# Where layer 0's later modulation vectors are made: five chunks on TensorE with summed tiles between them, three chunks at the feed-forward's entry

## The chip, the cores and the metric

The kernel runs on one core of a Trainium2 chip. The metric is the time of one execution in microseconds on the device. The engines that matter here are TensorE (PE in the profile, with PEld for its weight loads), VectorE (DVE), ScalarE (ACT), GpSimd (POOL) and SyncE (SP), whose queue issues most of the transfers. Each engine carries out its own list of instructions strictly in that list's order and waits at semaphores for the others.

## The reference, cut to what matters

Two transformer layers over 512 latent tokens and 256 context tokens, with a model width of 1024. Layer 0 has latent attention and neighbourhood attention side by side, layer 1 has sliding-window attention, and each is followed by a SwiGLU feed-forward. Every layer needs six modulation vectors of 1024 numbers for the latent stream (from `c`) and, in layer 0, as many again for the context stream (from `c_ctx`):

```python
for l in range(DEPTH):
    sh_a, sc_a, g_a, sh_f, sc_f, g_f = jnp.split(silu_c @ mod_w[l] + mod_b[l], 6, axis=-1)
    csh_a, csc_a, cg_a, csh_f, csc_f, cg_f = jnp.split(silu_cc @ mod_w[l] + mod_b[l], 6, axis=-1)
    a_lat = modulate(h_lat, sh_a, sc_a)            # rms_norm(h) * (1 + scale) + shift
    ...                                            # o_lat, o_ctx: the layer's attention and its output projection
    h_lat = h_lat + g_a * o_lat
    h_lat = h_lat + g_f * swiglu(modulate(h_lat, sh_f, sc_f), ffn_w_gate_up[l], ffn_w_down[l])
    ...                                            # the same for h_ctx while there is a layer after this one
return rms_norm(h_lat, final_norm)
```

In the order of that split the components are numbered 0 (attention shift), 1 (attention scale), 2 (attention gate), 3 (feed-forward shift), 4 (feed-forward scale) and 5 (feed-forward gate). Component (0, 3) is thus needed when the feed-forward of layer 0 modulates its input, and (0, 5) only when that feed-forward adds its output to the residual, far later.

## The kernel before, in words

All weights come in float32. A product with a weight tile is made of three matmuls on float32r parts: high weight by high data, high by low, low by high. ACT casts the high part of a weight tile (L332, in the feed-forward L1594), DVE subtracts it for the low part (L333, in the feed-forward L1595), and three PE lines of a helper (L345 to L347, L800 to L802, L1607 to L1609) make the products into PSUM tiles named `pss`, `psd`, `pst` and `pso`. A scheduler that simulates a timeline sets each engine's order from the program text; stretches of PE inside `in_order(...)` keep the order of the text.

The stages, with the time in the profiled execution at which each begins: the first modulation vectors and the entry norm; layer 0's input projections (60 us); the neighbourhood and the latent attention (184 us); the output projection and the norm that follows it; the feed-forward of layer 0, whose entry begins with the first gate-and-up products at 440 us and whose first down product is at 517.87 us; the rest of that feed-forward; layer 1; the last norm.

**The making of the modulation.** `all_mods` is a generator that makes one small piece at each step. `bg(n)` takes n steps of it; other work calls it at places that the text lists. `mod(...)` returns a finished vector and takes steps until it is there. There are three kinds of step:

- A PE chunk (`mods_pe`) makes 256 numbers of a component for both streams: four transfers of 256 KB from `mod_wp` on SP's queue into two `ph` and two `pl` tiles, matmuls with the conditioning (L202), an ACT copy (L204), matmuls that pick the two streams (L209), and two small DVE operations that add the bias (L216). Components (0, 4) and (0, 5) are made thus, in four chunks each.
- A summed tile makes 128 numbers in two steps. The first loads 256 KB into a `ph` and a `pl` tile and lets DVE multiply and sum them for the latent stream (L258). The second does that for the context stream by POOL (L275) and ACT (L276). Components (0, 2) and (0, 3) have 16 such tiles, 32 steps.
- A late tile is a single step, used from the end of the attention on: POOL's queue loads 512 KB (L229), in turn into one `rope` tile or into two `nb` tiles, and DVE sums (L236) and adds the bias (L241). Layer 1's components are made thus.

In the projections `bg` takes 37 steps in all (0.43 for each yield of the projections' loop, from the ninth on). Then it takes none until the output projection is done. In the feed-forward of layer 0, `bg(2)` is called at the second and third pair of gate-and-up blocks (j = 1 and 2), and `bg(more(j))` after that.

Before, the generator takes one PE chunk and then four summed steps, eight times over. The 37 steps of the projections thus hold all eight chunks and 29 of the 32 summed steps. Of the last three, one stands at the beginning of the attention; the last tile of (0, 3), number 7, is a late tile for both streams. Its two `nb` transfers are issued on POOL's queue at 256.56 us, and DVE works on it at the entry of the feed-forward. The four steps of j = 1 and 2 are then four late tiles of layer 1's component 1.

**The entry of the feed-forward.** `modulated_to` makes the input: DVE multiplies by the scale (L1533), ACT adds the shift (L1534), ACT and DVE split the result (L1594, L1595). The columns named "far" are begun before the norm's sum of squares is whole: `begun` starts products with `order[:4]` and `order[4:]` of the eight row blocks, the first with unnormalised data. The sum goes through `inverse`, a reciprocal (L1710) and `spread_to` (PE L474); then `norm.use` modulates the near columns, and the products of `near` run on PE in a written order. Pairs 1 to 3 follow. Weights of a pair are two `wr` tiles of 512 KB (one for gate, one for up) loaded by SP; a pair's sums and differences for a seven-product scheme (L1628, L1629, L1632, L1636 on DVE) go into `ph` and `pl` tiles, the same four-deep pools that the chunks and the summed tiles use. After the third pair `down0` begins with the first L345.

Of the kernel before, what the change touches and what calls it, by code (L numbers as in the profile page):

```python
# [102 lines left out]
def hybrid_kernel(ctx: ExitStack, tc, I, out):  # L103
# [189 lines left out]
    def component(l, comp):  # L293
        if (l, comp) in PE_MODS:
            yield from mods_pe(l, comp, PG if dense[0] else PQ)
            return
        for m in range(KT):
            yield from mod_tile(l, comp, m, (0, 1))

    def all_mods():  # L300
        by_pe, summed = (chain(component(0, a), component(0, b)) for a, b in ((4, 5), (2, 3)))
        for _ in by_pe:
            yield
            for _ in islice(summed, 4):
                yield
        yield from summed
        for comp in (1, 0):
            yield from component(1, comp)
        for comp in (2, 4, 3, 5):
            for m in range(KT):  # L310
                yield from mod_tile(1, comp, m, (0,))

    mods = all_mods()

    def bg(n=1):
# [1677 lines left out]
    norm, ops, sums, _ = combined(H, 1, 3, *HALVES)  # L1993
# [176 lines left out]
```

## Time and profile before

| | |
|---|---|
| median of 3 runs | 1563.93 us (1563.3 to 1567.26) |
| profiled execution | 1566.7 us, its span 1564.9 us |
| granted clock, mean | 0.992 |
| busy: PE, DVE, ACT, POOL | 97%, 75%, 52%, 18% of the span |
| projections, 60 to 184 us: PE busy | 123.22 of 124 us |
| entry of the feed-forward, 452 to 518 us: PE busy | 56.28 of 66 us |
| the longest wait of PE there | 5.74 us, ended at 457.75 us |

A row of the timeline reads: start in us, duration in us, engine, line, operation, output tile <- input tiles, shape; in square brackets the idle time of the engine ahead of it and what ended that. Neighbouring matmuls overlap in their ends, so the time that a matmul takes on PE is read from the distance of two starts. A row of the windows gives, for one stretch, its length, the busy time of PE, PEld, DVE, ACT and POOL with the number of instructions in brackets, the granted clock of PE as a share of full speed, the share of the transfer engines, and GB/s.

### The profile page before, as it was taken

To read this page: it belongs to the slowest core of one execution; us is meant where nothing else is said; L and a number is where in the kernel's file an instruction comes from. 1 tells how busy PE (TensorE), PEld (TensorE's weight loads), DVE (VectorE), ACT (ScalarE), POOL (GpSimd) and SP (SyncE) were. 2 spreads that over 40 slices of the span, in tenths; PEclk is the share of its full clock that TensorE was granted. 3 is DMA by queue.
4 is the path that set the end of the run, shared out by engine and by line. 5 is a ranking of instruction groups with operands and counts; after the bars stand their busy time and mean duration, and the time that the engine had idled before them with its cause. 6 is when DMAs were issued, how large, how long until landed. Compare 5 with 4: busy or idle time off the path is not lost.

```text
span 1564.9 us, 26627 instructions
## 1 busy us (share of the span) xinstructions
PE 1525.5 (97%) x9968; PEld 1358.2 (87%) x9968; DVE 1175.1 (75%) x2362; ACT 809.1 (52%) x1630; POOL 280.8 (18%) x317
## 2 busy tenths in 40 slices
PE   9999999999989999999999999999999999999998
PEld 6687767887988999898999999877789999898997
DVE  5896586666699497876877777888877679678686
ACT  5564587676564243242433345557757445354453
POOL 0264434332000010111111110381011000000000
PEclk9999999999999999999999999999999999999999
DMA  9585362004442554746666655140015223324222
GB/s 336 197 239 186 93 166 80 11 6 176 151 159 76 193 183 149 247 161 211 202 217 226 219 180 197 42 145 4 2 56 161 71 82 125 115 75 135 87 90 88
DMA packets 80849, 216.63 MB, mean 138 GB/s; under 512 B 10704, under 2 KB 17744, under 8 KB 80720
## 3 DMA queue, kind: packets, MB, share of 16 engines
q1 hardware_dynamic: 65200, 162.49, 32.2%
q0 software_dynamic: 13216, 49.29, 9.2%
q10 hardware_dynamic: 2304, 3.15, 0.5%
q8 instruction: 78, 1.28, 0.3%
q14 instruction: 51, 0.42, 0.1%
HBM read 187.10 MB, written 23.07 MB: 134 GB/s over the span
## 4 chain that ended last, share of the span: by engine, by line
PE 81%; DVE 8%; DMA 5%; issue 4%; ACT 2%; POOL 0%; SPq 0%; DVEq 0%; POOLq 0%; ACTq 0%
PE pso L557 5%; PE pss L345 4%; PE pss L346 4%; PE pss L347 4%; PE pss L1609 4%; PE psd L345 4%; PE pss L1607 4%; PE pss L1608 4%; PE psd L346 4%; PE psd L347 4%; PE psd L1609 3%; PE psd L1607 3%; PE psd L1608 3%; PE pss L789 3%; PE pst L504 3%
## 5 line engine op out<-in xcount | busy, mean ns | idle before, releaser
L332 ACT CAST wh<-wr 128x512 fp32r<-128x512 f32 (+2 forms) x139 | 105.9, 776 | 202.8 <-PE pss L346 64.5
L333 DVE TENSOR_TENSOR wl<-wr,wh 128x512 fp32r<-128x512 f32 (+2 forms) x136 | 126.3, 936 | 64.8 <-ACT wh L332 64.2
L563 ACT ACTIVATE p<-p,sm 128x512 f32<-128x512 f32 (+3 forms) x144 | 105.0, 730 | 27.7 <-DVE sm L567 26.7
L1607 PE MATMUL pss<-b,wh 128*128 128x384 f32 (+1 forms) x300 | 93.3, 311 | 0.0
L1608 PE MATMUL pss<-b,wh 128*128 128x384 f32 (+1 forms) x300 | 93.2, 311 | 0.0
L1609 PE MATMUL pss<-b,wl 128*128 128x384 f32 (+1 forms) x300 | 92.7, 312 | 0.0
L346 PE MATMUL psd<-b,wh 128*128 128x512 f32 (+3 forms) x249 | 84.3, 339 | 0.0
L1609 PE MATMUL psd<-b,wl 128*128 128x384 f32 (+1 forms) x248 | 78.9, 318 | 4.4 <-DVE wl L1595 4.4
L1608 PE MATMUL psd<-b,wh 128*128 128x384 f32 (+1 forms) x248 | 78.4, 316 | 0.0
L1607 PE MATMUL psd<-b,wh 128*128 128x384 f32 (+1 forms) x248 | 78.3, 316 | 0.0
L557 PE MATMUL pso<-ph,b 128*64 128x256 f32 (+1 forms) x400 | 76.9, 351 | 0.6 <-DVE ph L495 0.5
L557 PE MATMUL pso<-pl,b 128*64 128x256 f32 (+1 forms) x400 | 77.0, 351 | 0.1
L345 PE MATMUL psd<-b,wh 128*128 128x512 f32 (+3 forms) x209 | 73.6, 353 | 0.5 <-DVE b L495 0.5
L345 PE MATMUL pss<-st,wh 128*128 128x512 f32 (+2 forms) x212 | 72.6, 342 | 0.0
L347 PE MATMUL psd<-b,wl 128*128 128x512 f32 (+3 forms) x209 | 72.5, 348 | 0.0
L789 PE MATMUL pss<-st,st 128*128 128x512 f32 (+2 forms) x264 | 68.2, 372 | 4.3 <-DVE sm L567 4.1
L347 PE MATMUL pss<-st,wl 128*128 128x512 f32 (+2 forms) x212 | 72.2, 341 | 0.0
L346 PE MATMUL pss<-b,wh 128*128 128x256 f32 (+3 forms) x215 | 70.6, 329 | 0.0
L1594 ACT CAST wh<-ph 128x512 fp32r<-128x512 f32 x80 | 46.3, 619 | 44.8 <-DVE ph L1629 16.3
L1594 ACT CAST wh<-wr 128x1024 fp32r<-128x1024 f32 x40 | 42.0, 1050 | 42.0 <-PE pss L346 10.4
L1594 ACT CAST wh<-pl 128x512 fp32r<-128x512 f32 x80 | 46.0, 619 | 30.5 <-PE pst L1608 10.6
L504 PE MATMUL pst<-ident_r,p 128*128 128x128 f32 x346 | 57.8, 276 | 2.3 <-ACT p L563 1.2
(676 smaller groups left out, 5334.6 us busy)
## 6 DMA issues: line engine op xcount, KB each, us to landing
wr<-in_w_gu_dram SPq DMA_DIRECT2D x88, 512.0 KB, 4.1
wr<-in_w_out_dram SPq DMA_DIRECT2D x32, 512.0 KB, 3.7
wr<-in_w_dn_dram SPq DMA_DIRECT2D x64, 256.0 KB, 2.8
p<-home SPq DMA_DIRECT2D x40, 384.0 KB, 4.6
home<-p POOLq DMA_DIRECT2D x40, 384.0 KB, 4.6
nb<-in_mod_w_dram POOLq DMA_DIRECT2D x50, 256.0 KB, 3.6
rope<-in_mod_w_dram POOLq DMA_DIRECT2D x24, 512.0 KB, 3.9
wr<-in_w_in_dram SPq DMA_DIRECT2D x21, 512.0 KB, 4.3
```

Source lines behind the costliest of these rows:

```text
L332: S.copy(h, r)
L333: (G if eng else V).tensor_tensor(lo, r, f(h), op=ALU.subtract)
L345: PE.matmul(o, wh[:, k], mh[:, c], start=first and k == 0, stop=False)
L346: PE.matmul(o, wh[:, k], ml[:, c], start=False, stop=False)
L347: PE.matmul(o, wl[:, k], mh[:, c], start=False, stop=last and k == n - 1)
L557: ins = PE.matmul(o[64 * i : 64 * i + 64, c], v(kt), t, start=n == 0, stop=n == len(moving[i]) - 1)
L563: S.activation(p[:, c], p[:, c], AF.Exp, bias=nm, scale=-1.0, accum_out=dn)
L789: PE.matmul(o, x, k, start=i == 0, stop=i == 1)
L1594: S.copy(h, t)
L1607: PE.matmul(o, wh, xh, start=first and k == 0, stop=False, skip_group_check=not first)
L1608: PE.matmul(o, wh, xl, start=False, stop=False, skip_group_check=not first)
L1609: PE.matmul(o, wl, xh, start=False, stop=k == 3, skip_group_check=not first)
```

## The change

The turn in `all_mods` becomes one chunk and seven summed steps, for five chunks; the rest of the summed steps follow, and then the three chunks that are left.

```diff
         by_pe, summed = (chain(component(0, a), component(0, b)) for a, b in ((4, 5), (2, 3)))
-        for _ in by_pe:
+        for _ in islice(by_pe, 5):
             yield
-            for _ in islice(summed, 4):
+            for _ in islice(summed, 7):
                 yield
         yield from summed
+        yield from by_pe
         for comp in (1, 0):
             yield from component(1, comp)
```

Nothing else of the text is changed; from there on the lines of the file carry a number that is higher by one (L1595 before is L1596 now). The 37 steps of the projections now hold five chunks and all 32 summed steps, so component (0, 3) is whole when the attention begins. The steps of j = 1 and 2 at the feed-forward are now the last three chunks of (0, 5) and one late tile of layer 1, and each later late tile comes three steps later.

On DVE, at the entry of the feed-forward, ahead of the first products of the norm: `nb`, `cond` and `mod` in the rows of L236 are the late tile of (0, 3). Before:

```order
L1595 TENSOR_TENSOR pl_5303<-wr_5275,ph_5302 128x512
L236 ISA p_5013,mod_315_1519<-nb_5009,cond_67 128x512
L236 ISA mod_315_1519 128x1
L1710 RECIPROCAL sm_5060<-sm_5060 128x3
L236 ISA p_5015,mod_315_1519<-nb_5010,cond_67,mod_315_1519 128x512
L236 ISA mod_315_1519 128x1
L236 ISA p_5018,mod_316_1520<-nb_5009,cond_67 128x512
L236 ISA mod_316_1520 128x1
L241 SCALAR_TENSOR_TENSOR mod_315_1519<-mod_315_1519,modb_76 128x1
L1628 TENSOR_TENSOR pl_5411<-wr_5400 128x512
L236 ISA p_5020,mod_316_1520<-nb_5010,cond_67,mod_316_1520 128x512
L236 ISA mod_316_1520 128x1
```

Now, on DVE at the same place:

```order
L1596 TENSOR_TENSOR pl_5234<-wr_5206,ph_5233 128x512
L1589 TENSOR_TENSOR p_4994<-b_4685 128x384
L1589 TENSOR_TENSOR p_4999<-b_4772 128x384
L1589 TENSOR_TENSOR p_5004<-b_4859 128x384
L1589 TENSOR_TENSOR p_5009<-b_4945 128x384
L1711 RECIPROCAL sm_4991<-sm_4991 128x3
L1596 TENSOR_TENSOR st_4996<-p_4994,st_4996 128x384
L1596 TENSOR_TENSOR st_5001<-p_4999,st_5001 128x384
L1596 TENSOR_TENSOR b_5006<-p_5004,b_5006 128x384
L1596 TENSOR_TENSOR b_5011<-p_5009,b_5011 128x384
L1534 SCALAR_TENSOR_TENSOR p_5062<-b_4264,mod_183_848,pso_5026 128x384
```

The sums of the late tile and its two bias additions are gone from here, the split of pair 2 (L1628) stands later, and the norm's multiplications follow the reciprocal at once.

On SP's queue, the transfers of the weights at the same entry; `in_w_gu` is gate and up, `in_w_dn` is down, `in_mod_wp` is a chunk's weights. Before:

```order
L136 DMA wr_5399<-in_w_gu_dram 128x1024
L136 DMA wr_5400<-in_w_gu_dram 128x1024
L136 DMA wr_5554<-in_w_gu_dram 128x1024
L136 DMA wr_5555<-in_w_gu_dram 128x1024
L136 DMA wr_5689<-in_w_dn_dram 128x512
```

Now:

```order
L136 DMA ph_5268<-in_mod_wp_dram 128x512
L136 DMA pl_5270<-in_mod_wp_dram 128x512
L136 DMA wr_5359<-in_w_gu_dram 128x1024
L136 DMA wr_5527<-in_w_gu_dram 128x1024
L136 DMA ph_5272<-in_mod_wp_dram 128x512
L136 DMA pl_5274<-in_mod_wp_dram 128x512
L136 DMA ph_5292<-in_mod_wp_dram 128x512
L136 DMA pl_5294<-in_mod_wp_dram 128x512
L136 DMA ph_5296<-in_mod_wp_dram 128x512
L136 DMA pl_5298<-in_mod_wp_dram 128x512
L136 DMA wr_5528<-in_w_gu_dram 128x1024
L136 DMA wr_5662<-in_w_dn_dram 128x512
```

Twelve chunk transfers have come in (the last four stand behind these rows), two of them ahead of pair 2's second weight tile and six between pair 3's two.

On PE, in the same stretch, the products of pair 1's sums and of the far columns. Before:

```order
L1607 MATMUL pss_5357<-st_5065,wh_5280 128x384
L1608 MATMUL pss_5357<-st_5065,wh_5280 128x384
L1607 MATMUL psd_5308<-st_5231,wh_5280 128x384
L1608 MATMUL psd_5308<-st_5232,wh_5280 128x384
L1609 MATMUL psd_5308<-st_5231,wl_5281 128x384
```

Now, from the second half of one chunk's first transfers on:

```order
L202 MATMUL pst_5300<-pl_5294,cond_col_63 32x256 x2
L1608 MATMUL psd_5316<-st_4996,wh_5211 128x384
L1609 MATMUL psd_5316<-st_4996,wh_5211 128x384
L1608 MATMUL pst_5239<-st_5162,wh_5211 128x384
L1609 MATMUL pst_5239<-st_5163,wh_5211 128x384
L1610 MATMUL pst_5239<-st_5162,wl_5212 128x384
L1608 MATMUL pst_5239<-st_5169,wh_5211 128x384
L1609 MATMUL pst_5239<-st_5170,wh_5211 128x384
L1610 MATMUL pst_5239<-st_5169,wl_5212 128x384
L1608 MATMUL pst_5239<-b_5176,wh_5211 128x384
```

The chunk's matmuls now stand between those products. Row for row, the listing has 26 matmuls between the first and the second half of the first chunk, 36 from there to the second chunk, 11 to its second `ph` tile (`ph_5296`, the third row behind the ones shown), and 10 to its second `pl` tile.

## The prediction

> **What bounds the kernel now.** I read the clock and the engines first, then the chain, then windows over the stretches that the change touches, and last the timeline there.
>
> ```profile
> core 0: 1564.9 us, clock 0.992
> PE 1525.5 (97%) x9968; PEld 1358.2 (87%) x9968; DVE 1175.1 (75%) x2362; ACT 809.1 (52%) x1630; POOL 280.8 (18%) x317
> PE 81%; DVE 8%; DMA 5%; issue 4%; ACT 2%; POOL 0%; SPq 0%; DVEq 0%; POOLq 0%; ACTq 0%
> ```
>
> TensorE is busy for 97% of the span and is 81% of the chain that ended last, so work that leaves PE is time won, and beside it there are some 39 us (1564.9 - 1525.5) in which PE stands. The windows tell where the change meets either.
>
> ```profile
> core 0: us, PE busy (x) PEld busy (x) DVE busy (x) ACT busy (x) POOL busy (x), PEclk, DMA share, GB/s
> 80.00:100.00 20.00, 20.00 (x126) 16.81 (x125) 19.53 (x35) 11.46 (x26) 15.25 (x16) 1.00 0.74 216
> 100.00:120.00 20.00, 20.00 (x135) 16.26 (x134) 17.71 (x36) 12.92 (x30) 12.21 (x14) 1.00 0.94 264
> ...
> 160.00:180.00 20.00, 20.00 (x135) 16.22 (x133) 9.59 (x24) 10.32 (x24) 10.55 (x11) 1.00 0.34 106
> ...
> 452.00:456.00 4.00, 0.01 (x1) 0.00 (x0) 3.15 (x10) 1.36 (x3) 1.08 (x2) 0.92 0.65 252
> 456.00:460.00 4.00, 2.15 (x7) 1.65 (x8) 3.42 (x8) 3.31 (x7) 0.00 (x0) 0.50 0.22 70
> 460.00:462.00 2.00, 2.00 (x8) 2.00 (x8) 1.77 (x4) 1.49 (x4) 0.00 (x0) 0.50 0.00 0
> ...
> 486.00:490.00 4.00, 4.00 (x16) 4.00 (x15) 3.55 (x7) 0.01 (x1) 0.00 (x0) 0.57 0.65 230
> ...
> 452.00:518.00 66.00, 56.28 (x296) 54.50 (x296) 59.27 (x115) 36.34 (x67) 4.30 (x8) 0.92 0.32 105
> 518.00:560.00 42.00, 42.00 (x242) 37.74 (x241) 23.91 (x41) 10.46 (x18) 3.79 (x7) 1.00 0.54 183
> ```
>
> In the projections (the first three rows) PE never stands, but in the first two DVE is nearly full. From 452 to 518 us, the entry of the feed-forward, PE stands for 10 us and runs for nearly 8 us at half clock or little more; DVE is busy for 59.27 of 66 us. Behind that, PE is full and DVE has 43% to spare. The two chains of waits that make the entry long:
>
> ```profile
> 450.15 0.68 DVE L236 CUSTOM_DVE_ANT_0 p<-nb,cond 128x512 bf16<-128x512 f32 x1
> ...
> 453.17 0.69 DVE L1628 TENSOR_TENSOR pl<-wr 128x512 f32<-128x512 f32 x1 [0.85 <-DMA wr<-in_w_gu_dram]
> 453.78 0.74 DVE L236 CUSTOM_DVE_ANT_0 p<-nb,cond,mod 128x512 bf16<-128x512 f32 x1
> 454.45 1.49 DVE L1588 TENSOR_TENSOR p<-b 128x384 f32<-128x384 f32 x3
> ...
> 456.46 0.15 DVE L241 SCALAR_TENSOR_TENSOR mod<-mod,modb 128x1 f32<-128x1 f32 x1
> 456.65 0.51 ACT L1534 ACTIVATE b<-b,mod 128x256 f32<-128x256 f32 x1 [0.63 <-DVE mod L241]
> ...
> 457.75 0.69 PE L800 MATMUL pss<-b,wh 128*128 128x384 f32 x1 [5.74 <-ACT b L1594]
> ...
> 480.89 1.21 DVE L236 CUSTOM_DVE_ANT_0 p<-rope,cond 128x1024 bf16<-128x1024 f32 x1
> 482.03 1.22 DVE L236 CUSTOM_DVE_ANT_0 p<-rope,cond 128x1024 bf16<-128x1024 f32 x1
> ...
> 485.05 0.44 PE L1609 MATMUL psd<-b,wl 128*128 128x384 f32 x1 [1.93 <-DVE wl L1595]
> ```
>
> The first: PE's longest wait names ACT's cast L1594, but ACT waited for the shift (L1534 for `mod` of L241), and L241 is the last addition of the late tile of (0, 3), whose four sums began at 450.15 and stood behind a split that itself waited for weights. The second: a low part L1595 stands behind the two sums of a layer 1 tile in `rope`, and PE waits for 1.93 us.
>
> **The change, part by part.**
>
> *Three chunks leave the projections.* Their price on PE is read from the starts around one of them.
>
> ```profile
> 165.04 0.28 PE L347 MATMUL pst<-b,wl 128*128 128x258 f32 x1
> 165.25 0.41 PE L202 MATMUL pss<-ph,cond_col 128*32 128x256 f32 x2
> ...
> 166.48 0.28 PE L346 MATMUL pst<-b,wh 128*128 128x258 f32 x1
> 166.60 0.28 PE L347 MATMUL pst<-b,wl 128*128 128x258 f32 x1
> ...
> 170.14 0.39 PE L346 MATMUL pst<-b,wh 128*128 128x512 f32 x1
> 170.37 0.50 PE L209 MATMUL psd<-pick,p 128*128 128x2 f32 x4
> ...
> 171.05 0.40 PE L345 MATMUL pst<-b,wh 128*128 128x512 f32 x1
> 171.28 0.40 PE L346 MATMUL pst<-b,wh 128*128 128x512 f32 x1
> ```
>
> From L347 at 165.04 to L346 at 166.48 are 1.44 us, in which two products stand that take 0.12 each elsewhere (166.48 to 166.60): L202 costs 1.20. From L346 at 170.14 to L345 at 171.05 are 0.91 us for two products of 0.23 (171.05 to 171.28): L209 costs 0.45. A chunk is 1.65 us of PE, three are 4.95. PE never stands here, so all of it is won, if the attention begins earlier by it. What begins the attention is this:
>
> ```profile
> 183.67 0.69 ACT L457 ACTIVATE p<-psd,sm 128x512 f32<-128x512 f32 x1 [3.96 <-PE psd L347]
> ```
>
> ACT had stood for 3.96 us and waited for PE, so the start moves with PE. Term: -4.95. Three summed steps more come in. They bring DVE two sums and no PE; beside POOL's work such a sum takes up to four times its shortest:
>
> ```profile
> L258 DVE CUSTOM_DVE_ANT_0 p<-ph,cond x15: 664/687/2983, 79.0 to 173.3; 128x512 bf16<-128x512 f32 x15
> L258 DVE CUSTOM_DVE_ANT_0 p<-pl,cond,mod x15: 739/1652/2901, 79.8 to 175.7; 128x512 bf16<-128x512 f32 x15
> ```
>
> By the medians a tile is 0.69 + 1.65 = 2.34 us of DVE, by the longest 5.9. Summed steps now come at 7 of 8 in place of 4 of 5, 9% denser. From 80 to 120 us DVE has 40 - 37.24 = 2.76 us to spare, and 9% more of some six tiles there is 0.55 tiles, 1.3 us by the medians, 3.2 by the longest. I take no cost (the cover is those 2.76 us), and keep 0 to 0.5 (3.2 - 2.76) as its bounds; a weight split (L333) that comes late for PE would be what shows. SP has as many transfers fewer as leave with the chunks, so its queue gains.
>
> *The late tile of (0, 3) leaves the entry.* Its four sums and two additions no longer stand ahead of the shift. What is late next is the norm's own chain: four L1588 behind the last split at 450.15 take about 0.5 each (three in 1.49), then the reciprocal and the spread, so PE can be held until about 453 in place of 457.75: 4.7 of the 5.74 us go, with 1.0 kept. From 457.75 to 462 PE ran at a clock of 0.50 (4.25 us, so 2.1 us lost); that goes with the stall.
>
> *Layer 1's late tiles come three later.* The second wait, 1.93 us, goes with the `rope` sums ahead of it (now behind pair 3's sums), and so does its slow clock: 4 us at 0.57 are 1.7 lost. A late tile for both streams is 2.43 us of DVE by `rope` (two sums of 1.21 and 1.22) or 2.84 by `nb` (0.68 + 0.74, twice). Three of them leave the entry for the stretch behind 518 us, about 8 us, where DVE has 18 of 42 us to spare; at no cost there.
>
> *How much the entry can give.* At PE's spacing,
>
> ```profile
> 517.52 0.34 PE L1608 MATMUL pst<-b,wh 128*128 128x384 f32 x1
> ...
> 517.87 0.39 PE L345 MATMUL pss<-st,wh 128*128 128x512 f32 x1
> ```
>
> two matmuls of the entry are 0.35 us apart, 0.175 for one. The 296 of row 452 to 518 would take 51.8 us; they took 66.0, so 14.2 us are lost. From the rows above, the change takes away 4.7 + 2.1 + 1.9 + 1.7 = 10.4 of these. The 3.8 us that are left are small waits and the 1.0 kept.
>
> *Three chunks come to the entry.* On PE they cost 4.95 us, now in a stretch that PE sets once the stalls are gone. On DVE they bring six L216; less the four tiles gone (8 us, and 1.1 of the first), DVE falls from 59.3 to some 51 us, below PE's 51.8 + 4.95 = 56.75: PE is the bound. Unknown is what their transfers cost: twelve of 256 KB on SP's queue, with gate, up and down weights queued behind them. In the projections they landed thus (the issues for `ph`; then `pl`, chunks and summed tiles together):
>
> ```profile
> ph<-in_mod_wp_dram SPq DMA_DIRECT2D x10, 256.0 KB, 4.0
> ```
>
> ```profile
> DMA to landing us min/median/max: 2.5/4.1/6.9
> ```
>
> At the entry one `ph` and one `pl` slot are free for them, so a pair of transfers is issued when the L202 that read the pair before are done, and PE comes to its L202 after 26, 36 and 11 matmuls by the order: 4.55, 6.3 and 1.9 us. Against 4.1 this covers the first two and leaves 2.2 us of waiting at the second chunk's second half. The third chunk's slots come from pair 2's splits; I take it as covered. The nearest row for what such a wait does to the clock is the 1.93 us one, with 1.7 us lost behind it; half of that is 0.85. Behind the waiting L202 stand pair 1's products, and behind L216 on DVE pair 2's sums, a pair ahead of their use.
>
> [...]
>
> *Sum.* Entry: -10.4 + 4.95 + 2.2 + 0.85 = -2.4 with nothing of the other 3.8 us gained; -14.2 + 4.95 = -9.25 if PE ran without a gap, with no wait for weights. DVE begins the norm 6 us earlier there and has 8 us less to do, so some of the small waits behind its splits will go too: I take -4.5, nearer to the lower gain. With the projections: -4.95 - 4.5 = -9.5. Bounds: -14.2 and, with the denser steps' 0.5 and a whole 1.7 for the clock, -6.0. Against the profiled execution, 1566.7 - 9.5 = 1557.2; it stands 2.8 us above the median of its runs (1563.93), so the median after is 1554.4. I say 1554.5.
>
> **The rivals.**
>
> *The stall only moves.* With (0, 3) whole, another operand may end the same wait: the split L1628 still waited 0.85 us for weights at 453.17, and ACT has a row of casts. Then the entry gains the slow clock at most and pays for the chunks: about 0, and the whole -4.95, 1559. For it speaks that DVE was full there; against it that its 8 us less lie just ahead of the waits named.
>
> *The projections give nothing.* Either DVE falls behind with denser steps, or the attention, whose start the profile gives to PE, waits later for transfers and hands 4.95 back. Entry alone: 1559.4. Against it: PE stands in none of those three windows, and 2.76 us of DVE are free where it is fullest.
>
> *Slower: the chunk weights come late.* Place: the L202 at the entry. With a landing of d, PE waits d - 4.55, d - 6.3 and d - 1.9, and d - 4.0 at the third chunk if its slots leave one landing. At the longest, 6.9, these are 2.35 + 0.6 + 5.0 + 2.9 = 10.9 us, and three waits over 1.9 bring 5.1 of slow clock: 16.0 against the 9.25 that the entry can spare and the 4.95 of the projections, +1.8 us. L216 is held as long, and pair 2's sums stand behind it on DVE: if the 5.0 come again there, +6.8, 1570.7. It decides from a landing of about 6.5 us on. For it: PE cannot pass an L202. Against it: the median is 4.1, and the transfer engines were used at 0.32 of their time here against 0.74 and 0.94 in the projections.
>
> *The change does nothing*, if both parts are covered by the same later wait: 1564. No such wait stands behind 518 us, where PE is full.
>
> **How the numbers follow.** Both parts gained (1549.7 to 1558): 0.55. The stall moves (1559): 0.17. The projections give nothing (1559.4): 0.14. Slower by late weights: 0.11. Nothing: 0.03. About 0.3%, 4.7 us, is what a measurement can tell, so faster is below 1559.2: the first case, and half of the second and third, 0.71. Same: the other halves and the last, 0.18. Slower: 0.11. The range goes from 1548, the lower bound with some spread of the runs (1563.3 to 1567.26), to 1565; the slower case is left out of it.
>
> **What would show it.** Right: the attention's first L457 some 5 us earlier; 48 L202 instructions (three chunks of 16) gone from before 184 us and back between 450 and 500; no L236 ahead of the reciprocal; the wait of 5.74 us under 2; clock 1.00 from 456 to 462 as shifted; the first down product 8 to 11 us earlier. Waits of PE at L202 would show the weights late, waits of PE at L334 splits before 180 us the denser steps. The forecast is wrong if PE waits more than 5 us in sum at the three chunks, or if the shift (L1535) still waits for something other than the norm.

## The result and the profile after

The changed kernel has a median of 1554.59 us (1553.37 to 1555.36, 4 runs) against 1563.74 (4 runs); the ratio is 0.9936 with a 95% interval of 0.9919 to 0.9953. A second session gave 1555.12 us and 0.9941 (0.9928 to 0.9954). It is about 9 us faster; 1554.5 was forecast. The sum was right, but several of its terms were not; that it came within 0.1 us is luck, as shown below. The page after, by core, engine and chain:

```profile
core 0: 1551.6 us, clock 0.997
PE 1523.1 (98%) x9968; PEld 1353.7 (87%) x9968; DVE 1179.7 (76%) x2359; ACT 809.4 (52%) x1634; POOL 284.6 (18%) x317
PE 89%; DVE 6%; DMA 2%; ACT 1%; issue 1%; SPq 0%; DVEq 0%; ACTq 0%
```

PE's busy time has hardly changed (1525.5 to 1523.1), PE's idle time fell from 39 to 28.5 us, and the chain lies on PE for 89% in place of 81%. The waits of PE over the entry of the feed-forward, 440 to 508 us, after (us in all, times, the longest):

```profile
PE pss L1494 <- ACT p L378: 0.9, 1, 0.9
PE pst L1608 <- ACT p L1647: 0.8, 1, 0.8
PE pso L475 <- DVE sm L1711: 0.3, 1, 0.3
PE pst L1608 <- ACT wh L1595: 0.2, 1, 0.2
PE pst L1610 <- DVE wl L1596: 0.2, 1, 0.2
```

The 5.74 us wait and the 1.93 us wait are gone, and no row names a chunk's transfer. DVE at the same entry, after:

```profile
447.49 1.95 DVE L1589 TENSOR_TENSOR p<-b 128x384 f32<-128x384 f32 x4
449.36 0.17 DVE L1711 RECIPROCAL sm<-sm 128x3 f32<-128x3 f32 x1
...
451.30 4.28 DVE L1534 SCALAR_TENSOR_TENSOR p<-b,mod,pso 128x384 f32<-128x384 f32 x8
```

The norm's multiplications begin at 451.30, where before the first of them stood at 460.23, and no L236 stands ahead. The windows of after over that stretch (PE, PEld, DVE, ACT, POOL, granted clock, transfer share, GB/s):

```profile
450.00:460.00 10.00, 10.00 (x62) 9.04 (x61) 10.00 (x19) 9.84 (x16) 0.00 (x0) 1.00 0.27 100
...
442.00:508.00 66.00, 63.65 (x380) 56.69 (x379) 55.43 (x101) 37.55 (x69) 1.08 (x2) 1.00 0.40 133
```

PE is busy for 63.65 of 66 us at full clock, where before it was 56.28 of 66 at 0.92.

One profile is one execution, and the second profile of the kernel before (taken among the experiments) differs from the first by up to 2 us at one place. The two profiles of before (1566.7 and 1566.91 us) stand 2 to 3 us above the medians of that kernel, those of e6 and e7 3 to 4 above theirs, so differences of profiles come out larger than those of medians. The lengths below are differences of the starts of the same matmuls in each profile's timeline. The projections run from their first product (65.97 us in the first profile) to the first attention product (183.47); the attention from there to the last L1316 (363.69), the output and entry to the first down product (517.87), the rest of the feed-forward to the first sum of layer 1's norm (971.55), layer 1 to the last such sum (1556.30). The last column counts stretches of 3.4 us at a granted clock of 0.50 (half clock) between 60 and 1540 us (of which more below).

| kernel | projections | attention | output, entry | rest of feed-forward | layer 1 | half clock |
|---|---|---|---|---|---|---|
| before | 117.50 | 180.22 | 154.18 | 453.68 | 584.75 | 4 |
| before, again | 117.53 | 180.21 | 155.62 | 454.83 | 584.66 | 7 |
| after | 114.17 | 180.45 | 149.08 | 451.65 | 583.70 | 1 |
| after, again | 114.12 | 180.78 | 149.22 | 451.65 | 586.07 | 3 |
| e1 | 117.22 | 180.75 | 149.26 | 454.80 | 586.15 | 5 |
| e2 | 111.55 | 178.35 | 153.53 | 453.46 | 585.85 | 4 |
| e3 | 114.07 | 180.29 | 146.57 | 450.25 | 584.88 | 3 |
| e4 | 117.50 | 178.75 | 150.96 | 454.54 | 586.08 | 2 |
| e5 | 111.58 | 178.70 | 152.83 | 451.85 | 584.56 | 0 |
| e6 | 109.79 | 182.91 | 151.33 | 455.92 | 586.79 | 4 |
| e7 | 112.21 | 182.75 | 155.23 | 456.07 | 585.88 | 7 |
| e8 | 113.05 | 178.90 | 149.15 | 451.86 | 586.39 | 2 |
| e9 | 112.65 | 180.30 | 150.87 | 449.75 | 586.84 | 2 |
| e10 | 111.24 | 180.59 | 152.20 | 449.56 | 585.13 | 2 |

From before to after: projections -3.4, attention +0.2 to +0.6, output and entry -5.0 to -6.5, rest of the feed-forward -2.0 to -3.2, layer 1 -1.1 to +1.4.

### The profile page after: what moved, and what is told of

Same layout as the page of the kernel before. It is cut to its first block, busy times and chain, and to the rows that moved or that the text cites. A ratio compares the mean times of both kernels' runs of the same rounds, so it can differ in the third digit from the quotient of the medians.

```text
span 1551.6 us, 26660 instructions
## 1 busy us (share of the span) xinstructions
PE 1523.1 (98%) x9968; PEld 1353.7 (87%) x9968; DVE 1179.7 (76%) x2359; ACT 809.4 (52%) x1634; POOL 284.6 (18%) x317
## 4 chain that ended last, share of the span: by engine, by line
PE 89%; DVE 6%; DMA 2%; ACT 1%; issue 1%; SPq 0%; DVEq 0%; ACTq 0%
PE pso L558 5%; PE pss L1610 5%; PE pss L1608 5%; PE pss L346 5%; PE pss L1609 5%; PE pss L347 5%; PE pss L348 4%; PE psd L346 4%; PE psd L347 4%; PE psd L348 4%; PE psd L1610 3%; PE psd L1608 3%; PE psd L1609 3%; PE pst L1608 3%; PE pst L1610 3%; PE pst L1609 3%
## 5 line engine op out<-in xcount | busy, mean ns | idle before, releaser
L334 DVE TENSOR_TENSOR wl<-wr,wh 128x512 fp32r<-128x512 f32 (+2 forms) x136 | 126.3, 934 | 67.2 <-ACT wh L333 59.3
L1609 PE MATMUL pss<-b,wh 128*128 128x384 f32 (+1 forms) x302 | 93.6, 310 | 0.0
L1610 PE MATMUL pss<-b,wl 128*128 128x384 f32 (+1 forms) x302 | 92.8, 310 | 0.0
L347 PE MATMUL psd<-b,wh 128*128 128x512 f32 (+3 forms) x237 | 80.9, 341 | 0.0
L347 PE MATMUL pss<-b,wh 128*128 128x512 f32 (+3 forms) x239 | 79.8, 334 | 0.0
L1608 PE MATMUL psd<-b,wh 128*128 128x384 f32 (+1 forms) x226 | 70.8, 313 | 0.0
L1609 PE MATMUL psd<-b,wh 128*128 128x384 f32 (+1 forms) x226 | 70.7, 313 | 0.0
L1610 PE MATMUL psd<-b,wl 128*128 128x384 f32 (+1 forms) x226 | 70.6, 313 | 0.0
L346 PE MATMUL psd<-b,wh 128*128 128x512 f32 (+3 forms) x197 | 70.1, 356 | 0.2 <-DVE b L496 0.2
L348 PE MATMUL psd<-b,wl 128*128 128x512 f32 (+3 forms) x197 | 69.1, 352 | 0.0
L1595 ACT CAST wh<-ph 128x512 fp32r<-128x512 f32 x80 | 46.3, 620 | 42.9 <-PE pss L1609 13.1
L348 PE MATMUL pss<-b,wl 128*128 128x512 f32 (+3 forms) x183 | 63.7, 348 | 0.0
L346 PE MATMUL pss<-b,wh 128*128 128x512 f32 (+3 forms) x183 | 63.1, 353 | 0.0
L1595 ACT CAST wh<-wr 128x1024 fp32r<-128x1024 f32 x40 | 42.0, 1050 | 40.4 <-PE pss L347 10.2
```

What stands on the lines that cost most here:

```text
L334: (G if eng else V).tensor_tensor(lo, r, f(h), op=ALU.subtract)
L346: PE.matmul(o, wh[:, k], mh[:, c], start=first and k == 0, stop=False)
L347: PE.matmul(o, wh[:, k], ml[:, c], start=False, stop=False)
L348: PE.matmul(o, wl[:, k], mh[:, c], start=False, stop=last and k == n - 1)
L1595: S.copy(h, t)
L1608: PE.matmul(o, wh, xh, start=first and k == 0, stop=False, skip_group_check=not first)
```

## The experiments

### The two kernels again

The kernel before, once more:

> The kernel before, unchanged, for a second profile. The two profiles at hand differ by 1.6 us within the first 26 us, before anything that the change touches, and by 2.3 us between 518 and 882 us, of which a PE wait of 1.96 us at 661.98 is the largest piece. Theory: the first is a difference between executions, the second belongs to the kernel's order. Then this profile has the 5.74 us wait at about 457 and a wait of some 2.0 us at about 661 again, while the matmul that began at 26.67 may begin anywhere from 25.0 to 26.7. Rival: the wait at 661 is a late transfer of one execution; then it is absent or under 1 us here.

One run, 1566.91 us. Its first row of PE's waits over the entry, and the matmul that waits later:

```profile
PE pss L800 <- ACT b L1594: 5.7, 1, 5.7
```

```profile
661.55 0.69 PE L1609 MATMUL psd<-b,wl 128*128 128x384 f32 x1 [2.16 <-DVE wl L1595]
```

Both waits belong to the kernel's order, and the matmul that began at 26.67 began 2.07 us earlier here, at 24.60, a little below the 25.0 that the expectation allowed: differences ahead of the projections are between executions.

The changed kernel, once more:

> The changed kernel, unchanged, for a second profile and more runs beside the kernel before. In the profiles so far each half-clock stretch of PE lasts 3.4 us and costs 1.7, and the kernel before has five or six of them between 60 us and its last norm, the changed one has one (149 to 154 us). Theory (work, waits and 1.7 us for each such stretch make the time): the same median, 1554.6 +- 1.5, ratio 0.993 to 0.995, and this profile again has one to three stretches; whether the 2.05 us wait at about 1037 is followed by one may differ. Rival (the first profile was a lucky one): 1557 or more.

1555.12 us (1553.37 to 1556.67, 5 runs), as expected, with three half-clock stretches (0.50 for 3.4 us from 150.9, 191.9 and 1038.4 us). PE did wait for the weights of one chunk, the third, in this execution:

```profile
486.75 0.62 PE L202 MATMUL psd<-ph,cond_col 128*32 128x256 f32 x4 [0.60 <-DMA ph<-in_mod_wp_dram]
```

### The stall alone, the chunks alone (e1, e2)

e1 is the kernel before with

```diff
-DBG = 0.43
+DBG = 0.465
```

> The kernel before with 40 steps in the projections in place of 37 (0.465 per yield): component (0, 3) is finished there as in the changed kernel, but all eight chunks stay in the projections and none comes to the feed-forward; the late tiles stand as before. Theory (the gain is of two parts that add): the 5.74 us wait and its half clock go, about 7 us; the 1.93 us wait of late tiles at the entry and the 2 us wait at about 661 stay, in the same or another place; the projections cost up to 1.5 us more for three summed steps in them. Sum -5 to -7, 1557 to 1559. Rival (the stall only makes way for another one): -2 or less. Rival (the whole gain of the changed kernel is the stall): -9, 1554.6.

1561.97 us, ratio 0.9982 (0.9969 to 0.9995), -2.8 us. The entry became 5 to 6.4 us shorter, nearly as much as after. The projections took no more for three more summed steps (117.22 us). Two waits of PE at L1609 are still there:

```profile
479.19 0.45 PE L1609 MATMUL psd<-b,wl 128*128 128x384 f32 x1 [2.04 <-DVE wl L1595]
...
656.97 0.44 PE L1609 MATMUL psd<-b,wl 128*128 128x384 f32 x1 [2.74 <-DVE wl L1595]
```

Both stayed, as the theory of two parts had it, each with half clock behind it (0.50 from 480.3 to 483.7 us and from 657.8 to 661.2). The gain of the median is 2 us short of the theory's range, and layer 1, which the edit does not touch, took 1.4 us more in this execution.

e2 is the changed kernel with

```diff
-DBG = 0.43
+DBG = 0.395
```

> The changed kernel with 34 steps in the projections in place of 37 (0.395 per yield): five chunks and 29 summed steps there, so three chunks leave the projections for the feed-forward's entry as in the changed kernel, but the last tile of (0, 3) is a late tile at the entry again, as before. Theory: the projections give 3.3 to 5 us; the wait of some 5.7 us with its half clock stays at the entry, and the three chunks cost 4.95 us of PE behind it, less what late tiles leave there (the 1.93 us wait and its clock 1.7, and the wait at 661, about 2). Sum -2 to -5, 1559 to 1562. Rival (chunks fill PE's stall at the entry, so they cost nothing there): -7 or more, 1557 or less. Rival (chunks only change places): 0.

1557.57 us, ratio 0.9951 (0.9939 to 0.9964), -7.6 us. This is the larger part, and larger than the theory allowed. By its size it is the first rival, but the chunks do not fill the stall: their first matmul (L202) runs at 457.05 us, and the stall ends at 447.64. In the profile the projections are 6.0 us shorter, 1.7 of them for a half-clock stretch (3.4 us at 0.50) that this execution did not have there, and the attention 1.9; why the attention is shorter was not tried. The entry keeps a wait that is 1.5 us shorter, with its half clock (0.50 from 445.5 to 452.3 us):

```profile
PE psd L801 <- ACT b L1595: 4.2, 1, 4.2
```

In medians the parts add, as far as can be told: -2.8 and -7.6 are -10.4, against -9.2 for both, and each of the two is known to 2 us either way.

### What the chunks cost at the entry (e3)

```diff
         yield from summed
-        yield from by_pe
+        for c in range(1, 4):
+            for v in range(2):
+                for k in (2 * c, 2 * c + 1):
+                    MOD[0, 5, v, k] = MOD[0, 4, v, k]
+            yield
```

> The changed kernel without the last three chunks: their three steps are taken but make nothing, and six columns of component (0, 5) are those of (0, 4). This leaves out 12 transfers, 48 L202, the L209, three ACT copies and six L216 at the entry; all else keeps its step. Theory (PE bounds the entry once the stall is gone): the chunks cost their work on PE, 4.95 us, and no more; this kernel is 4.5 to 5.5 us faster than the changed one, 1549 to 1550. Rival (the chunks fill gaps that other waits would leave): 0 to 2.5 us faster, 1552 to 1554.6. Rival (they hold back other work too, through slots and SP's queue): over 6 us faster, under 1548.6.

1551.74 us, ratio 0.9918 (0.9903 to 0.9934), some 3 us faster than the changed kernel, of which the entry gives 2.5 to 2.7 (149.08 and 149.22 to 146.57). That is nearest to the rival of filled gaps, whose 2.5 us it exceeds a little. Without the chunks PE waits at the entry for more (in this kernel the line numbers are higher by four):

```profile
PE pss L1731 <- ACT b L374: 0.8, 2, 0.6
PE pst L1612 <- ACT p L1651: 0.8, 1, 0.8
PE pst L1612 <- ACT p L1658: 0.8, 1, 0.8
PE psd L1612 <- ACT wh L1599: 0.6, 1, 0.6
...
```

With the two rows of 0.4 and 0.3 at the norm and two of 0.2 these are 4.1 us; with the chunks they are 2.4. So 1.7 of the chunks' 4.95 us stood where PE would have waited.

### The stall removed otherwise (e4, e5)

e4 is the kernel before with one line at the end of the attention, behind `late.append(...)`:

```diff
+    mod(0, 3, 1, 7)
```

> The kernel before with one line more: mod(0, 3, 1, 7) at the end of the attention, so the late tile of (0, 3) is summed on DVE while the latent attention runs out (about 355 to 370 us) and no longer at the feed-forward's entry. The projections are untouched. Theory (the stall is worth what it costs at the entry, whoever removes it): from the end of the attention to the first down product 5.5 to 7 us less, as in e1, up to 1 us lost at the end of the attention; sum -3 to -6 against before. Rival (the time at the entry is given back behind 518 us): 0 to -2, with PE waits at L1609 there longer than the 2 us of before.

1565.18 us, ratio 0.9999 (0.9986 to 1.0012): no gain. The profiled execution (1561.60 us) has the entry 3.2 to 4.7 us shorter, and new waits of 1.5 and 1.2 us between 367 and 375. Its eleven runs lie in two groups, four at 1560.3 to 1561.6 and seven at 1564.8 to 1569.6. The profile is of the first group; what the second does was not seen. Behind 518 us the wait at L1610 is 2.79 us, in place of 1.96 before, as the rival had it.

e5 is e2 with the same line:

> e2 (34 steps in the projections, three chunks at the entry) with the line of e4: both parts of the change, but the three summed steps that the changed kernel adds to the projections are not in them. From the profiles of e2 and of the changed kernel, the projections and the neighbourhood attention of e2 are 4.7 us shorter, its way from there to the first down product 4.5 us longer. Theory (the three more summed steps cost some 2.6 us of the projections and 2 us of the attention, the stall is removed as well by e4's line): 3 to 5 us faster than the changed kernel, 5 to 7 faster than e2, -13 to -15 against before. Rival (the two parts overlap, the end of the attention pays for the tile): as the changed kernel within 1.5 us, -9 to -11.

1555.06 us, ratio 0.9947 (0.9935 to 0.9959): the rival. The projections keep e2's gain, and the entry gives it back ahead of its begin. PE's largest waits from 350 to 508 us in e5:

```profile
PE psd L346 <- DVE ph L496: 2.4, 1, 2.4
PE pso L558 <- DVE ph L496: 1.0, 1, 1.0
```

DVE copies of the attention's last block (L496) stand behind the tile's four sums, and the last of them also behind a weight split (L334) that took 3.07 us there, against 1.21 for the next one.

### Four chunks at the entry (e6, e7)

e6 is the changed kernel with

```diff
-        for _ in islice(by_pe, 5):
+        for _ in islice(by_pe, 4):
             yield
-            for _ in islice(summed, 7):
+            for _ in islice(summed, 8):
```

and 36 steps; e7 is e5 with four chunks (seven summed steps behind each, as in e5) and 33 steps.

> The changed kernel with one chunk less in the projections: four chunks with eight summed steps each, 36 steps (0.418 per yield), and four chunks at the entry, all four steps of j = 1 and 2; late tiles one step later again. Theory (e3: a chunk at the entry costs 0.8 to 0.9 us there since it fills gaps; a chunk leaving the projections gives at most 1.65, less what denser summed steps take): between -1 and +1 us against the changed kernel. Rival (each chunk moved is worth the same as the first three, 3.35 / 3 = 1.1 less 0.85): -0.3. Rival (PE waits for the fourth chunk's transfers or pair 3 waits behind it): +2 or more.

> e5 with one chunk less in the projections: four chunks and 29 summed steps, 33 steps (0.385 per yield), four chunks at the entry, the tile of (0, 3) at the end of the attention. Theory: 0.8 us faster than e5 (1.65 in the projections less 0.85 at the entry), at most 2; if the summed steps bound the projections by then, 0 to +1. Against before -13 to -16.

e6 has 1560.04 us, ratio 0.9977 (0.9968 to 0.9987); e7 has 1563.93, ratio 0.9993 (0.9984 to 1.0002). Both are 5 us or more slower than the five-chunk kernels they come from; every expectation missed. The projections of e6 are as short as they should be, 109.79. The loss begins with the attention:

```profile
185.34 0.69 DVE L568 CUSTOM_DVE_ANT_1 wr<-pss,nb 128x512 f32<-128x512 f32 x1 [2.26 <-DMA nb<-in_nb_dram]
```

```profile
PE pss L790 <- DVE sm L568: 6.7, 5, 2.4
```

These rows are DVE's longest wait and PE's first row from 170 to 250 us, both of e6. DVE waits for a bias tile of the attention: its transfer is issued at 180.33, and DVE can begin 5.0 us later; in the changed kernel it is issued at 182.10 and DVE begins 3.1 us later. PE waits twice for 2.4 us, and half clock follows both times (0.50 from 186.0 to 189.5 us and from 192.9 to 196.3). Why that transfer is late in these two was not tried. A second loss is of the late tiles: with a fourth chunk they come one step later again, and the wait behind 518 us, gone in the changed kernel, is back with its half clock (0.50 from 657.1 to 660.5 us):

```profile
657.02 0.66 PE L1610 MATMUL psd<-b,wl 128*128 128x384 f32 x1 [2.02 <-DVE wl L1596]
```

In e7 it is 2.20 us, at 661.34, with 0.50 from 661.7 to 665.1. On DVE the two sums of a `rope` tile and one of an `nb` tile stand ahead of the low part in both, as before the change, and the rest of the feed-forward is 4.3 to 4.4 us longer than in the changed kernel. No row of the entry of e6 names a chunk's transfer.

### A version that is faster (e8, e9, e10)

e8 is e2 with the late tile called from the output projection instead of the attention's end:

```diff
                 if m >= wait:
                     next(rest, None)
+                if l == 0 and i == 0 and m == 2:
+                    mod(0, 3, 1, 7)
                 bg(units[i])
```

> e5 with the late tile of (0, 3) placed elsewhere: mod(0, 3, 1, 7) is called in the output projection, after its third block, so DVE sums it at about 385 to 395 us, where it is busy for 55 to 60%, and not at the end of the attention, where e5 made PE wait 1.0 + 2.4 us. Theory (e5 lost what it gained in the projections to those waits): 3 to 4 us faster than e5 and than the changed kernel, 1551 to 1552, ratio 0.991 to 0.9925; no PE wait of over 1 us between 355 and 395. Rival (the change's order is as good as any, losses come back elsewhere): as e5, 0.9947.

1552.42 us (1551.94 to 1553.41), ratio 0.9924 (0.9912 to 0.9937), 2.7 us faster than the changed kernel in the same session (the intervals of the two ratios overlap, the runs hardly: 1551.94 to 1553.41 against 1553.37 to 1556.67). No wait of over 1 us is left from 355 to 508. From 385 to 395 us DVE is now busy for 9.52 of 10 us in place of 6.42, and PE for all 10 in both. The first and the last of the tile's four sums:

```profile
390.48 0.68 DVE L236 CUSTOM_DVE_ANT_0 p<-nb,cond 128x512 bf16<-128x512 f32 x1
...
396.30 0.75 DVE L236 CUSTOM_DVE_ANT_0 p<-nb,cond,mod 128x512 bf16<-128x512 f32 x1
```

e9 is the changed kernel with its 24 one-column matmuls in two groups of twelve. The calls, cut to what matters (the function now makes one group at a time):

```diff
-            if x == ROOTS_AT:
-                latent_roots(accs)
+            if x in "56":
+                latent_roots(int(x) - 5, *accs[int(x) - 5])
```

> The changed kernel with the 24 one-column matmuls of L1163 (146.8 to 149.9 us, the sums of squares of the latent attention) cut in two: twelve as before, twelve after the next block of the projection. Nothing is left out. Theory (3 us of one-column matmuls count as idle for the clock, and half clock follows): no half-clock stretch at 149 to 154 us, projections 1.7 us shorter (112.5 from the first product to the attention, in place of 114.2), 1.7 us faster than the changed kernel, 1552.9. Rival (the clock falls there for another reason, e.g. the phase of some window): the stretch stays, no difference.

> e8 and e9 together. Theory: the sum of both, if e8's projections have the half-clock stretch (e2's did not, e5's neither: then no gain from the cut): 0 to 1.7 us faster than e8, 1549.5 to 1552. Rival (the cut moves the attention's start, since the latent columns come later): 1 us slower than e8 or more.

In e9's profile the half clock behind these matmuls is gone and the projections are 112.65 us, as expected. The windows around the two halves, e9:

```profile
148.00:151.00 3.00, 3.00 (x27) 2.95 (x26) 3.00 (x4) 2.81 (x7) 2.36 (x3) 1.00 0.27 87
151.00:155.00 4.00, 4.00 (x27) 3.60 (x26) 3.93 (x8) 3.16 (x8) 2.53 (x2) 1.00 0.50 131
158.00:160.00 2.00, 2.00 (x17) 1.88 (x16) 2.00 (x4) 1.05 (x4) 2.00 (x2) 1.00 0.18 58
160.00:164.00 4.00, 4.00 (x30) 3.77 (x30) 3.31 (x9) 2.83 (x10) 1.92 (x2) 1.00 0.67 199
```

Yet the time is 1556.41 us, ratio 0.995 (0.9936 to 0.9964), no better than the changed kernel (0.9941): the output and entry are 1.7 us longer in its profile, with one wait of 1.40 us at 470.03 in place of 0.80. e10 has 1553.28 us, ratio 0.9924 (0.9909 to 0.9938), the same as e8 and 1.3 us above the end of its expected range: in the profiles its projections are 1.8 us shorter than those of e8, and its output and entry 3 us longer.

## Why the prediction was right, term by term

**Three chunks leave the projections: -4.95 forecast, -3.4 found.** The attention did begin 4.98 us earlier (L458 at 178.69), but 1.6 of that lie ahead of the projections and are the execution's. What PE pays is a wait at a chunk that stayed, ACT's copy being late behind the denser summed steps:

```profile
102.00 0.61 PE L209 MATMUL pst<-pick,p 128*128 128x2 f32 x4 [1.16 <-ACT p L204]
```

The term for the denser steps had 0 to 0.5 and asked whether DVE had room. This wait is most of the missing 1.6. The engine that was late is ACT, which the forecast did not look at. In e2, with three summed steps fewer, the same wait is 0.25 us. The other 0.4 fit a chunk that is worth 1.5 us and not 1.65: with this wait counted back in, and 1.7 taken off where only before has a half-clock stretch in the projections, three chunks leave 4.5 us in the changed kernel and in e2, and four leave 6.0 in e6, which has no such wait.

**The stall at the entry: -4.7 and -2.1 forecast, confirmed.** e1 and after both lose it and its half clock (1.00 from 440 to 480 us in both), whoever finishes (0, 3). Forecast and measured are hard to part beyond that, since other waits went too.

**The second wait: -1.9 and -1.7 forecast, confirmed.** After, no wait of PE for a low part is over 0.2 us at the entry, and e1, which leaves the late tiles where they were, keeps the wait (2.04) and its half clock (0.50 from 480.3 us).

**Transfers of the chunks: +2.2 and +0.85 forecast, 0 to 0.6 found.** This term was mis-sized. Landing times at the entry, from the view of the `ph` tiles of after:

```profile
DMA to landing us min/median/max: 2.5/2.7/4.3
```

The `pl` tiles landed in 3.5 (median). For the same kind of transfer the projections of before have 4.1 and 4.3, so their rows were the wrong ones to price it by; the load beside it is the likely reason, an estimate from the shares in use. The transfer engines were in use for 0.32 of the time at the entry before and for 0.40 after, against 0.74 and 0.94 in the windows of before from 80 to 120 us; the forecast had these rows and used them only in a rival. The pair that was priced at 2.2 is there as the order had it: the second chunk's second pair is issued at 469.39, and its L202 runs at 472.53, without a wait. That is 3.14 us where 1.9 was forecast, and 0.80 of it is a wait of PE for ACT (L1647, ended at 470.76), so a part of the cover is luck. The 0.6 us of the second profile are at the third chunk, which the forecast took as covered. The slower rival needed landings of 6.5 us.

**Three chunks at the entry: +4.95 forecast, +2.5 to 2.7 found** (e3), since they fill gaps in part. DVE is busy for 55.43 of the 66 us, where 51 was forecast, and PE is the bound as forecast. The output and entry in all gave 5.0 to 6.5 us, where -4.5 was taken and -2.4 to -9.25 were the bounds. The first down product begins 9.85 us earlier (508.02), inside the 8 to 11 that was to show it, but 1.65 of that lie ahead of the projections.

**Behind the entry: 0 forecast, -2.0 to -3.2 found.** The prediction moved the late tiles there at no cost and did not see that they stood in the way. The wait of L1609 on the low part L1595 is absent after. In the profile of before it is this row:

```profile
661.98 0.45 PE L1609 MATMUL psd<-b,wl 128*128 128x384 f32 x1 [1.96 <-DVE wl L1595]
```

On DVE before, the low part stands behind three sums of late tiles, of which the first is a `rope` tile:

```profile
657.81 1.22 DVE L236 CUSTOM_DVE_ANT_0 p<-rope,cond 128x1024 bf16<-128x1024 f32 x1
...
658.95 1.22 DVE L236 CUSTOM_DVE_ANT_0 p<-rope,cond 128x1024 bf16<-128x1024 f32 x1
...
660.10 0.69 DVE L236 CUSTOM_DVE_ANT_0 p<-nb,cond 128x512 bf16<-128x512 f32 x1
...
660.71 1.22 DVE L1595 TENSOR_TENSOR wl<-wr,wh 128x1024 fp32r<-128x1024 f32 x1
```

With the late tiles three steps on, one sum of an `nb` tile stands there after, and L1596 follows at 649.27 in that profile:

```profile
648.66 0.68 DVE L236 CUSTOM_DVE_ANT_0 p<-nb,cond 128x512 bf16<-128x512 f32 x1
...
649.27 1.22 DVE L1596 TENSOR_TENSOR wl<-wr,wh 128x1024 fp32r<-128x1024 f32 x1
```

e1, with the late tiles where they were, keeps the wait (2.74), and e3, which shifts them as the change does, has none over 0.5 us there. It is a matter of which tile meets that place: one step further on (e6, e7) the `rope` tile and the wait are back. Nor are late tiles alone in it: e2 has the single `nb` sum there and still a wait of 1.34 us; its DVE had waited 2.53 us for weights at 645.05, against 1.03 after.

So the sum came out by terms that cancel, which is luck: 1.6 too much in the projections and 0.2 to 0.6 in the attention, 0.5 to 2 too little at the entry, 2 to 3 not seen behind it. None of the rivals happened; the one of the projections, with ACT in place of DVE, did so to a third.

## What to carry to other kernels

Price a transfer by rows from a stretch with the same load on the transfer engines, not by the row with the same name (here 2.7 and 3.5 us at a share of 0.40, where 4.1 was taken, from the projections with 0.74 and 0.94 in their fullest windows). When background work is shifted by some steps on an engine that here kept the order of its list (on DVE before, the sum listed behind the split that waited 0.85 us for weights began behind it, at 453.78), go through every place where such a step stands ahead of something the bound engine waits for; here that was worth as much as a named term, and one step more (e6, e7) brought the wait back. Before moving a late operand, place its producer in a stretch where its engine has gaps and nothing waits behind it: 2.7 us more came from the output projection (e8), none from the attention's end (e5).

## What the runs showed of the hardware

Between 60 and 1540 us PE's granted clock falls to 0.50 for stretches of 3.41 us (149.70 to 153.12 in the first profile of after), at times two end to end (455.34 to 462.16 in the first of before). Where PE has work throughout, such a stretch holds 1.7 us less of it, an estimate from these two figures. One execution differs from another of the same kernel by several of them (four and seven in the two profiles of before). Two things stood ahead of them in the fourteen profiles, idle time of PE and matmuls of one column, and most of the stretches are told by how much of these lay in one window of a grid.

The grid is seen from the starts of the stretches, read in slices of 0.01 us. In the second profile of before they begin at 152.93, 453.30, 484.02, 490.85, 661.52 and 1050.64 us: from the first, 88, 97, 99, 149 and 263 times 3.4133 us. In each of the thirteen profiles with two or more stretches (those at the very beginning and end counted) the starts lie such whole multiples apart, to within 0.01 us, and the place of the grid changes from execution to execution: in the two profiles of after the nearest edges to 1038 us are at 1037.17 and at 1038.41.

Stretches follow most of the short waits, not all. Of 29 waits of PE of 1.8 to 2.8 us between 60 and 1540 us in the fourteen profiles, 22 were followed by one. The grid sorts most of them. Of its windows at full clock, all 21 in which PE was idle for 1.92 us or more were followed by half clock, 12 of the 19 with 1.50 to 1.89 us, and none of the 36 with 1.0 to 1.49. Of those with less, ten were: nine with one-column matmuls (below), and one in e10 with a wait of 0.78 us and twelve such matmuls. The same wait at 1038 us in the two profiles of after (2.05 and 2.07 us) was followed by none in the first and by one in the second. In the first an edge of the grid cuts it, in the second it lies in one window. The windows of the grid, first profile, then second:

```profile
1033.76:1037.17 3.41, 1.93 (x15) 1.42 (x13) 3.41 (x9) 1.44 (x4) 3.41 (x3) 1.00 0.23 90
1037.17:1040.58 3.41, 2.70 (x14) 1.91 (x14) 3.41 (x13) 2.74 (x7) 3.33 (x3) 1.00 0.93 309
```

```profile
1034.99:1038.41 3.42, 1.35 (x8) 0.76 (x7) 3.42 (x8) 0.88 (x3) 3.42 (x3) 1.00 0.27 85
1038.41:1041.82 3.41, 3.41 (x12) 2.75 (x11) 3.23 (x11) 3.18 (x8) 3.33 (x4) 0.50 0.90 330
```

Stretches follow one-column matmuls too, with PE busy by the profile. After, PE ran 24 of them and L209 from 146.77 to 149.91 us, and then:

```profile
146.00:149.00 3.00, 3.00 (x25) 2.82 (x25) 3.00 (x4) 2.97 (x6) 2.36 (x2) 1.00 0.32 87
149.00:150.00 1.00, 1.00 (x10) 1.00 (x9) 0.97 (x3) 0.82 (x3) 1.00 (x2) 0.85 0.11 14
150.00:153.00 3.00, 3.00 (x15) 3.00 (x15) 3.00 (x4) 2.33 (x5) 2.04 (x2) 0.50 0.88 190
```

Of the twelve profiles with the 24 together, nine have such a stretch right behind them; e9 and e10, with twelve and twelve, have none there. It is not their number alone: in e2 24 of them in a row (144.28 to 146.87) had none behind them, in e1 24 in a row (149.09 to 151.69) had one. Here too the windows tell them apart. In the nine, matmuls of one or two columns fill 1.89 to 3.04 us of the window ahead of the stretch; in the other three (e2, e5, e6) an edge of the grid cuts the 24, and no window has more than 1.78 us of them; in e9 and e10 none has more than 1.70.
